# A two-block transformer kernel on one core: its state space mixer in chunks of four tokens, with states at chunk ends and outputs by block matrices

## The chip, the cores and the metric

The kernel runs on one core of a Trainium2 chip. TensorE (PE in the views, PEld for its weight loads) multiplies matrices, VectorE (DVE) and ScalarE (ACT) work on elements, GpSimd (POOL) does a few fills, and SyncE (SP) issues the transfers from HBM. Each engine takes its instructions in order and waits on semaphores where it needs another's result. The metric is the device time of one execution in microseconds, the median of several runs.

## What is computed

256 tokens of width 2048 go through two blocks. The first one has a state space mixer beside a dilated attention, then a feed-forward part; the second one has two kinds of attention and a Fourier mixer. All of it is float32. The mixer takes 1024 of the channels as 64 groups of 16, and each group drives 64 complex states:

```python
bu_re = jnp.einsum('bsgc,gnc->sbgn', uf, bbar_re)
bu_im = jnp.einsum('bsgc,gnc->sbgn', uf, bbar_im)
_, _, h_re, h_im = lax.associative_scan(
    _complex_linear_combine, (a_seq_re, a_seq_im, bu_re, bu_im), axis=0)
y = (jnp.einsum('sbgn,gcn->bsgc', h_re, c_re.astype(f32))
     - jnp.einsum('sbgn,gcn->bsgc', h_im, c_im.astype(f32))
     + d.astype(f32) * uf)
y = jax.nn.gelu(y.reshape(B, S, SSM_WIDTH))
return y * jax.nn.sigmoid(y @ w_glu.astype(f32))
```

So h[t] = a·h[t-1] + B·u[t] for every state, and y[t] = Re(C·h[t]) + d·u[t]. The factor a does not depend on t.

## The kernel before

Nearly all time goes to matrix products whose weights are read once from HBM. A product either runs in float32 (two matmul records in the trace for one 128x512 product) or is split into a high and a low part and run as three products of a faster kind (one record each). The high part is a cast on ACT (`split`, line 177), the low part a subtraction on DVE (line 178).

The side work is written as generators, `Lane`s. A main loop calls `tick()` after every weight tile, and each lane is advanced by its rate in the table `T`: `ada=1.8` and `ssm=5` of a lane's own units at each tick. `ada` streams the modulation weights through DVE (`ada_add`, line 278), one 0.5 MB tile a unit. `ssm` is the mixer. The program order that results is then arranged for each engine by the framework's scheduler, so that rows of different lanes alternate.

Two stages matter here. In stage A (90 to 211 us) the input projection runs, while the modulation columns that it needs are still being computed group by group of channels; the mixer prepares its constants up to the mark "prep". In stage B (211 to 457 us) the rest of the q, k and v products, the dilated attention and one product with w_out run (`rest`, `scores`, `values`, `gemm_full`), and the mixer does its recurrence. At the end of stage B `lanes["ssm"].finish()` stands ahead of the gate product (`ssm_w_glu`), which needs the mixer's y.

The mixer before works on half of the groups (16 pairs of groups, 128 state rows a pair) and 128 tokens at a time, so in four runs:

- `products` (lines 590 to 612) and `expand_b` make, for the taps j = 0 to 3, the matrices a^j·B, transposed so that one matmul sums four tokens.
- `load` (652) copies u for all tokens and all four shifts to `ssm_us`; `inputs` (666) does 32 matmuls of 128x128 weights and 128 columns and copies the result to `ssm_h`. It holds, for each token, the sum of the last four inputs with their powers of a.
- `scan` (676) is then h[t] = a^4·h[t-4] + that sum: 32 steps of four tokens, four DVE instructions of 128 elements each (two products into `ssm_tq`, line 682, two sums into `ssm_h`, line 684).
- `outputs` (689) multiplies every state by C: 32 matmuls with 128x32 weights (`ssm_cl`, made by `expand_c`, 634) and 128 columns, into four column strips; line 698 adds d·u.

## Time and profile before

| | us |
|---|---|
| median of three runs | 2488.83 |
| lowest, highest run | 2485.3, 2496.29 |
| the profiled execution | 2486.17 |
| its span, first to last instruction | 2484.4 |
| PE busy in the span | 2352.2 (95%) |
| DVE busy in the span | 1810.1 (73%) |
| ACT busy in the span | 1124.0 (45%) |
| read from HBM in the span | 587.19 MB, 237 GB/s |

A busy share of the whole span is a mean over stages with different limits. The change lies in the first 460 us, and what it is worth has to be read there: which engine is full in that stretch, and what the idle pieces of that engine waited for.

### The profile page before, as it was taken

What the parts mean: (1) busy time and instruction counts of PE and PEld (TensorE: products, weight loads), DVE (VectorE), ACT (ScalarE), POOL (GpSimd) and SP (SyncE); (2) the same over time, 40 slices, a digit from 0 to 9 for tenths busy, and PEclk for the clock granted to TensorE, in tenths of its full rate; (3) what the DMA queues carried; (4) which work ended last, traced back from release to release, by engine and by line L of the source; (5) the groups of instructions that cost most, each with busy time, mean ns of one, the idle gap of its engine ahead of it and who ended that gap; (6) DMA issues with size and microseconds to landing.
All of it is one profiled execution on the core that took longest, in us unless ns stands there. A gap on an engine that the chain in (4) does not pass through costs nothing.

```text
span 2484.4 us, 30494 instructions
## 1 busy us (share of the span) xinstructions
PE 2352.2 (95%) x10855; PEld 1800.0 (72%) x10855; DVE 1810.1 (73%) x3054; ACT 1124.0 (45%) x1745; POOL 1.4 (0%) x12
## 2 busy tenths in 40 slices
PE   5899999989999999999999999999997999999997
PEld 3455554668887878778777888777776778888886
DVE  5877998787778899876778789646678655555557
ACT  3227752454444333344355455555435445444442
POOL 0000000000000000000000000000000000000000
PEclk9899999999999999999999999999998999999999
DMA  9888778768888878888877988624473765665664
GB/s 290 309 296 307 231 260 285 253 224 291 286 278 273 297 267 291 266 270 280 266 250 222 306 282 291 210 89 162 136 262 115 231 200 176 193 194 157 177 210 138
DMA packets 291538, 591.35 MB, mean 238 GB/s; under 512 B 33733, under 2 KB 56617, under 8 KB 291385
## 3 DMA queue, kind: packets, MB, share of 16 engines
q1 hardware_dynamic: 291384, 589.40, 73.1%
q8 instruction: 85, 1.39, 0.2%
q14 instruction: 69, 0.56, 0.1%
HBM read 587.19 MB, written 2.13 MB: 237 GB/s over the span
## 4 chain that ended last, share of the span: by engine, by line
PE 47%; DMA 22%; DVE 20%; issue 5%; ACT 4%; SPq 1%; DVEq 0%; ACTq 0%
PE mm L133 39%; DMA raw<-in_ada_w_dram 15%; DVE wl L178 6%; DVE acc L278 6%; PE at L133 4%; PE tp L133 2%; DMA raw<-in_w_in_attn_dram 2%; DMA raw<-in_w_ada_dram 2%; ACT ssm_us L663 1%; ACT wh L177 1%; DMA raw<-in_w_ffn_down_dram 1%; PE tp L189 1%; DVE ssm_h L684 1%; DVE ssm_tq L682 1%; DVE wa L278 1%
## 5 line engine op out<-in xcount | busy, mean ns | idle before, releaser
L133 PE MATMUL mm<-wh,s 128*128 128x512 f32 (+3 forms) x4768 | 1462.9, 386 | 2.3 <-ACT wh L177 2.1
L177 ACT CAST wh<-raw 128x1024 fp32r<-128x1024 f32 (+3 forms) x642 | 655.9, 1023 | 896.8 <-PE mm L133 669.9
L133 PEld LDWEIGHTS mm<-wh,s 128*128 128x128 f32 x4768 | 890.2, 189 | 181.1 <-issue 7.8
L178 DVE TENSOR_TENSOR wl<-raw,wh 128x1024 fp32r<-128x1024 f32 (+3 forms) x642 | 755.2, 1185 | 316.6 <-ACT wh L177 311.9
L133 PE MATMUL mm<-wl,s 128*128 128x512 f32 (+3 forms) x2384 | 920.4, 386 | 21.4 <-DVE wl L178 19.6
L278 DVE SCALAR_TENSOR_TENSOR acc<-raw,condT,acc 128x1024 f32<-128x1024 f32 (+2 forms) x413 | 477.7, 1164 | 208.8 <-DMA raw<-in_ada_w_dram 141.9
L133 PEld LDWEIGHTS mm<-wl,s 128*128 128x128 f32 x2384 | 450.5, 189 | 119.7 <-DVE wl L178 33.2
L133 PE MATMUL mm<-wh,sl 128*128 128x512 f32 x608 | 230.9, 475 | 5.1 <-ACT sl L753 2.8
L133 PEld LDWEIGHTS mm<-wh,sl 128*128 128x128 f32 x608 | 112.5, 191 | 68.2 <-issue 41.8
L133 PE MATMUL mm<-wl,sl 128*128 128x512 f32 x368 | 158.2, 494 | 2.6 <-DVE wl L178 2.5
L133 PEld LDWEIGHTS mm<-wl,sl 128*128 128x128 f32 x368 | 67.7, 189 | 52.8 <-issue 38.1
L684 DVE TENSOR_TENSOR ssm_h<-ssm_h,ssm_tq 128x128 f32<-128x128 f32 x256 | 73.2, 286 | 2.5 <-ACT ssm_h L673 1.0
L133 PE MATMUL at<-wl,sl 128*128 128x512 f32 x152 | 68.3, 597 | 1.1 <-DMA wl<-in_w_in_dram 0.5
L133 PE MATMUL tp<-wc,sl 128*128 128x128 f32 (+1 forms) x352 | 49.2, 293 | 18.8 <-ACT wc L837 15.1
L133 PEld LDWEIGHTS tp<-wc,sl 128*128 128x128 f32 x352 | 44.7, 198 | 29.0 <-ACT wc L837 15.4
L682 DVE TENSOR_TENSOR ssm_tq<-ssm_h,ssm_co 128x128 f32<-128x128 f32 x248 | 61.3, 286 | 1.8
L278 DVE SCALAR_TENSOR_TENSOR wa<-raw,condT,wa 128x512 f32<-128x512 f32 (+1 forms) x75 | 48.1, 641 | 11.6 <-DMA raw<-in_w_ada_dram 10.8
L133 PEld LDWEIGHTS at<-wl,sl 128*128 128x128 f32 x152 | 27.7, 190 | 38.7 <-issue 28.6
L133 PE MATMUL at<-s,s 128*128 128x512 f32 (+1 forms) x96 | 42.0, 616 | 3.7 <-ACT wd L1317 3.0
L133 PEld LDWEIGHTS at<-ssm_us,ssm_bl 128*128 128x128 f32 x256 | 30.6, 191 | 11.6 <-ACT ssm_h L673 5.7
L133 PE MATMUL at<-ssm_us,ssm_bl 128*128 128x128 f32 x256 | 34.0, 283 | 3.2 <-ACT ssm_h L673 1.4
L663 ACT COPY ssm_us<-sl 32x512 f32<-32x512 f32 (+3 forms) x56 | 34.4, 615 | 0.9
(330 smaller groups left out, 1588.8 us busy)
## 6 DMA issues: line engine op xcount, KB each, us to landing
raw<-in_w_ada_dram SPq DMA_DIRECT2D x192, 512.0 KB, 5.3
raw<-in_ada_w_dram SPq DMA_DIRECT2D x192, 512.0 KB, 4.8
raw<-in_w_in_fourier_dram SPq DMA_DIRECT2D x128, 512.0 KB, 4.2
raw<-in_w_ffn_gate_dram SPq DMA_DIRECT2D x88, 512.0 KB, 5.0
raw<-in_w_ffn_up_dram SPq DMA_DIRECT2D x88, 512.0 KB, 4.8
raw<-in_w_ffn_down_dram SPq DMA_DIRECT2D x88, 512.0 KB, 5.3
raw<-in_w_in_attn_dram SPq DMA_DIRECT2D x72, 512.0 KB, 5.1
raw<-in_w_out_fourier_dram SPq DMA_DIRECT2D x64, 512.0 KB, 4.2
```

What stands on the lines that cost most here:

```text
L133: PE.matmul(o, l, r, start=start, stop=stop)
L177: S.copy(hi, src)
L178: V.tensor_sub(lo, src, hi.bitcast(F32))
L189: PE.transpose(b[:, o:o + 128], src(c0 + c, t), ident)
L278: V.scalar_tensor_tensor(out=acc, in0=raw, scalar=c, in1=acc, op0=ALU.mult, op1=ALU.add)
L663: copy(d[:, :, z:NT], uT[half][32 * i:32 * i + 32, :, t0 + z - j:t0 + NT - j])
L682: V.tensor_tensor(out=tq, in0=prev[:, c:c + 1].to_broadcast([128, 2, 16, 4]), in1=cof[:, c].unsqueeze(3).to_broadcast([128, 2, 16, 4]), op ...
L684: V.tensor_tensor(out=cur, in0=cur, in1=tq, op=ALU.add)
```

## The change

Both halves of the groups now go through one recurrence, and it keeps only the state at the end of each chunk of four tokens, 64 chunks in all. For that, `chunked` lays u out as 4 tokens x 32 channels on the partitions and 64 chunks in the free dimension, and `inputs` does 64 matmuls of 64 columns in all (128 of 128 columns before). A `scan` step is one product of 128 elements and two sums of 64, with 63 steps in place of 128. Since the states inside a chunk are not there any more, an output needs two things: the chunk's own inputs through a block matrix `tk` of 4x4 blocks C·a^k·B (with d on the diagonal), and the state at the end of the chunk before through the matrices C·a^(j+1), `gx`. `kernel_of` computes the blocks with 32 matmuls for each half (weights 128x128, 32 columns), `chunk_kernel` copies them into place, `outward` and `outward_powers` make C and its powers, and `outputs` does three matmuls of 64 or 63 columns for each of the 32 pairs, with 128x128 weights, and copies the result back to token order in 64 copies of 32 partitions. `products` and `kernel_of` of both halves, and `outward`, now stand ahead of the mark "prep", in stage A. The rates in `T` and everything outside the mixer are as before.

```diff
+        def products(half):
+            pr = slab([128, 4, 256])
+            ex = exs[half] = [w8([128, 16, 4, 2, 16]) for _ in range(2)]
...
+            for j in range(4):
+                d = [pr[:, 2 * (j % 2) + comp] for comp in range(2)]
...
+                for comp in range(2):
+                    for g in range(2):
+                        S.activation(out=ex[comp][:, :, 3 - j, g], in_=f(d[comp]), func=AF.Copy,
+                                     scale=maskb[:, g:g + 1])
+                yield 2.0
+        def outward():
+            for comp in range(2):
+                for half in range(2):
+                    cx = w2([128, 4, 2, 64], "wb")
...
+                    for kk in range(4):
+                        PE.transpose(b[:, kk * 128:(kk + 1) * 128], cx[:, kk].rearrange("p g n -> p (g n)"), ident)
...
+        def kernel_of(half):
...
+            b = ps_at()
+            for q in range(16):
+                for comp in range(2):
+                    mm(b[:, 32 * q:32 * q + 32], exs[half][comp][:, q].rearrange("p j g c -> p (j g c)"),
+                       ct[comp][:, q].rearrange("p g c -> p (g c)"), comp == 0, comp == 1)
...
+        def chunked(half):
+            us[half] = slab([128, 16, 64])
+            for i in range(4):
+                for q in range(4):
...
+                    copy(d, uT[half][32 * q:32 * q + 32, :, i:256:4])
         def inputs(half):
+            for comp in range(2):
+                for h8 in range(2):
+                    b = ps_at()
+                    for q in range(8):
+                        mm(b[:, q * 64:(q + 1) * 64], bls[half][comp][:, 8 * h8 + q], us[half][:, 8 * h8 + q], True, True)
+                    g0 = 16 * half + 8 * h8
+                    S.copy(st[:, :, comp, g0:g0 + 8].rearrange("p n g -> p g n"), b.rearrange("p (g n) -> p g n", g=8))
+        def scan():
+            for c in range(1, 64):
+                cur, prev = st[:, c], st[:, c - 1]
+                tq = sp.tile([128, 2, 2, 32], F32, name=uname("ssm_tq"), tag="ssm_tq")
+                V.tensor_tensor(out=tq, in0=prev.unsqueeze(1).to_broadcast([128, 2, 2, 32]), in1=co, op=ALU.mult)
+                for i in range(2):
+                    V.tensor_tensor(out=cur, in0=cur, in1=tq[:, :, i], op=ALU.add)
+                yield 0.7
+        def outward_powers():
+            for half in range(2):
...
+                for j in range(4):
+                    t1, t2 = temp(), temp()
+                    V.tensor_tensor(out=f(t1), in0=gi, in1=ai, op=ALU.mult)
...
+                            S.activation(out=gx[half][comp][:, :, j, g], in_=g_, func=AF.Copy, scale=maskb[:, g:g + 1])
+        def outputs(half):
+            for h8 in range(2):
+                b = ps_at()
+                for q in range(8):
+                    g = 8 * h8 + q
+                    o = b[:, q * 64:(q + 1) * 64]
+                    mm(o, tk[:, half, g].rearrange("p j c -> p (j c)"), us[half][:, g], True, False)
+                    for comp in range(2):
+                        mm(o[:, 1:64], gx[half][comp][:, g].rearrange("p j g c -> p (j g c)"),
+                           st[:, 0:63, comp, 16 * half + g], False, comp == 1)
                 for i in range(4):
+                    for q in range(4):
+                        copy = (S.copy, V.tensor_copy)[q % 2]
+                        copy(uT[half][32 * q:32 * q + 32, 2 * h8:2 * h8 + 2, i:256:4],
+                             b[32 * i:32 * i + 32].rearrange("p (k q n) -> p q k n", k=2, q=4)[:, q])
+                yield 2.0
+        yield from outward()
+        for half in range(2):
+            yield from products(half)
+            yield from kernel_of(half)
+            if half == 0:
+                yield from expand_b(0)
+        yield "prep"
...
+        for c, cost in enumerate(scan()):
+            yield cost
+            if c % 8 == 2:
+                next(powers, None)
+                yield 2.0
+            if c in (20, 40):
+                chunk_kernel(c // 20 - 1)
...
+        for half in range(2):
+            yield from outputs(half)
```

Where the new work stands is decided by the scheduler, and three places of its order are of use. The first is on PE in stage A, between the 128x512 products of two q, k and v tiles (an `at` buffer is a PSUM bank, `wl` a weight tile). Before:

```order
L133 MATMUL at_801<-wl_847,sl_208 128x512
L133 MATMUL at_802<-wl_847,sl_208 128x512
L133 MATMUL at_859<-wl_861,sl_195 128x512
L133 MATMUL at_860<-wl_861,sl_195 128x512
L133 MATMUL at_859<-wl_871,sl_208 128x512
L133 MATMUL at_860<-wl_871,sl_208 128x512
```

and now, where `wb` is `ct`, `ssm_w` the matrices of `products`, and two rows stand for sixteen pairs of them:

```order
L133 MATMUL at_852<-wl_908,sl_208 128x512
L133 MATMUL at_853<-wl_908,sl_208 128x512
L133 MATMUL at_866<-wb_860,ssm_w_673 128x32
L133 MATMUL at_866<-wb_863,ssm_w_674 128x32
...
L133 MATMUL at_920<-wl_922,sl_195 128x512
L133 MATMUL at_921<-wl_922,sl_195 128x512
```

The 32 matmuls of the first `kernel_of` stand two weight tiles ahead of the end of this group of channels, and they take one of the two `at` banks; those of the second one stand behind the first product of the last group, with no boundary behind them.

The second place is on PE at the mixer's last outputs. Before, they stand inside the first products of the gate (`mm_3698`, whose weights `wh_3702` and `wl_3703` are `ssm_w_glu`), and thirty-two of them follow each other:

```order
L133 MATMUL mm_3698<-wh_3702,sl_3689 128x512
L133 MATMUL mm_3699<-wh_3702,sl_3689 128x512
L133 MATMUL mm_3698<-wl_3703,sl_3689 128x512
L133 MATMUL at_3219<-ssm_h_2412,ssm_cl_2819 32x128
L133 MATMUL at_3219<-ssm_h_2412,ssm_cl_2829 32x128
...
L133 MATMUL mm_3698<-wh_3702,sl_3690 128x512
```

Now, the products with the powers (`ssm_w`) and with the block matrices (the second `ssm_h`) stand among the v products of the second half of the heads:

```order
L133 MATMUL mm_2738<-wh_2824,sl_221 128x512
L133 MATMUL at_2312<-ssm_h_1379,ssm_w_1681 128x63
L133 MATMUL at_2312<-ssm_h_1379,ssm_w_1682 128x63
L133 MATMUL at_2312<-sl_1384,ssm_h_1380 128x64
...
L133 MATMUL mm_2739<-wh_2824,sl_221 128x512
L133 MATMUL mm_2646<-raw_2819,cz 32x512 x2
```

They moved ahead of the second four heads and of the product with w_out, and the whole recurrence has to be done before them. The third place is DVE inside the recurrence, before:

```order
L684 TENSOR_TENSOR ssm_h_2412<-ssm_h_2412,ssm_tq_2910 128x32x4
L684 TENSOR_TENSOR ssm_h_2412<-ssm_h_2412,ssm_tq_2913 128x32x4
L682 TENSOR_TENSOR ssm_tq_2916<-ssm_h_2412,ssm_co 128x128
L682 TENSOR_TENSOR ssm_tq_2919<-ssm_h_2412,ssm_co 128x128
L684 TENSOR_TENSOR ssm_h_2412<-ssm_h_2412,ssm_tq_2916 128x32x4
```

and now:

```order
L713 TENSOR_TENSOR ssm_tq_2280<-ssm_h_1379,ssm_co 128x128
L278 SCALAR_TENSOR_TENSOR acc_2636<-raw_2821,condT,acc_2636 128x1024
L715 TENSOR_TENSOR ssm_h_1379<-ssm_h_1379,ssm_tq_2280 128x64 x2
L713 TENSOR_TENSOR ssm_tq_2284<-ssm_h_1379,ssm_co 128x128
L715 TENSOR_TENSOR ssm_h_1379<-ssm_h_1379,ssm_tq_2284 128x64 x2
```

A step has three instructions that each need the one before, where it had two pairs; `ada_add` (line 278) still stands in between.

## Rows read from the trace of the kernel before

**Rows 1.** Engine busy time by stretch, stages A, B and the rest

```profile
core 0: us, PE busy (x) PEld busy (x) DVE busy (x) ACT busy (x) POOL busy (x), PEclk, DMA share, GB/s
90.00:211.00 121.00, 113.97 (x342) 60.22 (x341) 90.48 (x169) 31.86 (x64) 0.37 (x3) 0.96 0.89 305
211.00:457.40 246.40, 236.90 (x1156) 123.69 (x1154) 222.60 (x797) 136.48 (x312) 0.58 (x4) 0.99 0.79 270
```

**Rows 2.** PE in time inside stage B: start, length, instruction, count

```profile
267.30 3.60 PE L133 MATMUL mm<-wl,sl 128*128 128x512 f32 x8
270.74 7.03 PE L133 MATMUL mm<-wh,sl 128*128 128x512 f32 x16
```

**Rows 3.** What PE waited for in stage B: us, times, longest

```profile
PE tp L189 <- ACT sl L937: 1.6, 2, 1.3
PE at L133 <- ACT ssm_h L673: 1.4, 2, 1.0
PE tp L317 <- ACT wc L314: 0.8, 1, 0.8
```

**Rows 4.** Groups of stage B: count | busy us, mean ns | idle before

```profile
L133 PE MATMUL at<-ssm_us,ssm_bl 128*128 128x128 f32 x256 | 34.0, 283 | 3.2 <-ACT ssm_h L673 1.4 <-issue 0.5 <-DVE sl L698 0.5
L133 PE MATMUL at<-ssm_h,ssm_cl 128*32 128x128 f32 x256 | 9.7, 311 | 0.0
L644 PE MATMUL tp<-ident,wb 128*128 128x128 f32 x16 | 2.3, 276 | 0.0
L682 DVE TENSOR_TENSOR ssm_tq<-ssm_h,ssm_co 128x128 f32<-128x128 f32 x248 | 61.3, 286 | 1.8
L684 DVE TENSOR_TENSOR ssm_h<-ssm_h,ssm_tq 128x128 f32<-128x128 f32 x256 | 73.2, 286 | 2.5 <-ACT ssm_h L673 1.0
L278 DVE SCALAR_TENSOR_TENSOR acc<-raw,condT,acc 128x1024 f32<-128x1024 f32 x52 | 66.4, 1279 | 7.9 <-DMA raw<-in_w_ada_dram 7.8
L604 DVE TENSOR_TENSOR sl<-sl,ssm_t 128x256 f32<-128x256 f32 x4 | 1.7, 423 | 0.0
```

**Rows 5.** DVE in time, one recurrence step and its neighbours

```profile
445.69 0.61 DVE L684 TENSOR_TENSOR ssm_h<-ssm_h,ssm_tq 128x128 f32<-128x128 f32 x2
446.33 0.49 DVE L682 TENSOR_TENSOR ssm_tq<-ssm_h,ssm_co 128x128 f32<-128x128 f32 x2
446.74 0.61 DVE L684 TENSOR_TENSOR ssm_h<-ssm_h,ssm_tq 128x128 f32<-128x128 f32 x2
```

**Rows 6.** DVE, the nearest smaller instruction, from the groups of 90 to 130 us

```profile
L580 DVE TENSOR_TENSOR ssm_p<-ssm_ptmp 128x32 f32<-128x32 f32 x1 | 0.2, 183 | 0.0
```

**Rows 7.** Weight loads in time, for matmuls of one column

```profile
164.62 0.97 PEld L133 LDWEIGHTS tp<-ones,wa 128*128 128x128 f32 x8 [1.20 <-ACT acc L301]
```

**Rows 8.** PE in time in stage A

```profile
97.93 3.70 PE L133 MATMUL at<-wh,sl 128*128 128x512 f32 x8 [0.25 <-DVE sl L800]
112.78 7.13 PE L133 MATMUL at<-wl,sl 128*128 128x512 f32 x16 [0.43 <-DVE sl L800]
164.65 1.02 PE L133 MATMUL tp<-ones,wa 128*128 128x1 f32 x8 [1.15 <-DVE col L748]
169.01 0.79 PE L133 MATMUL mm<-wh,ssm_h 128*128 128x512 f32 x1 [3.34 <-ACT ssm_h L177]
```

**Rows 9.** Busy time and granted clock of one short stretch of stage A

```profile
167.00:175.00 8.00, 5.82 (x15) 4.15 (x16) 7.86 (x14) 6.25 (x13) 0.00 (x0) 0.57 0.80 242
```

**Rows 10.** PE in time at the third and last outputs of the mixer

```profile
405.39 2.02 PE L133 MATMUL at<-ssm_h,ssm_cl 128*32 128x128 f32 x64
...
451.59 0.74 PE L133 MATMUL mm<-wh,sl 128*128 128x512 f32 x2 [1.21 <-ACT wh L177]
453.47 0.51 PE L133 MATMUL mm<-wl,sl 128*128 128x512 f32 x1 [1.14 <-DVE wl L178]
453.90 3.61 PE L133 MATMUL at<-ssm_h,ssm_cl 128*32 128x128 f32 x64
```

## What the change was predicted to do

> **What bounds the kernel now.** I read the busy time by stretch first. The change is inside two stages: A, 90 to 211 us, and B, 211 to 457.4 us. In B, PE is busy 236.9 of 246.4 us and DVE 222.6; transfers run at 270 GB/s there and at 305 GB/s in A [rows 1]. So two engines are nearly full in B, and the share of the whole span would not have told that. A busy PE is not yet a PE at its peak, so next comes PE in time: 8 records of 512 columns start within 3.44 us (267.30 to 270.74) and 16 take 7.03 [rows 2], 0.43 us a record, and this rate returns wherever such products follow each other. PE is thus the engine that sets the end of B, and only its idle 9.5 us (246.4 - 236.9) and a few slow pieces can be taken back by making others faster. Then come its waits: short ones, behind ACT, DVE and transfers, the longest 1.3 us [rows 3]. DVE carries the recurrence, 61.3 + 73.2 = 134.5 us, beside 66.4 us of modulation sums [rows 4]; a step takes 445.69 to 446.74 = 1.05 us [rows 5], 128 steps 134 us.
>
> **DVE, part by part.** A new step has one product of 128 elements and two dependent sums of 64. A 128-element instruction costs 0.25 to 0.29 us (61.3/248, and 73.2/256) [rows 4], one of 32 elements 0.18 [rows 6], so I take 0.22 for 64 elements, and 0.25 + 2 x 0.22 = 0.69 us a step; 63 steps make 43 us, up to 0.8 and 50 us if nothing stands between dependent ones. `outward_powers` adds 48 instructions like line 604, 0.42 us each [rows 4], 20 us, and the copies some 10. DVE's mixer work in B falls from 134.5 to 73-80 us. What that is worth on the clock is only what PE waited for.
>
> **PE in stage B.** Two kinds of product go. The old `inputs` held PE for 34.0 us and the old `outputs` for 9.7 [rows 4]; `expand_c` (16 transposes, 2.3 us of busy time [rows 4], 1.8 us one behind the other) goes to stage A as `outward`. What comes is 64 matmuls of `inputs` and 96 of `outputs`, all with 128x128 weights and at most 64 columns. No row has this shape. Its columns alone would take half of a 128-column record: 34.0/256 = 0.133 us with its waits, so 0.067. The other bound is the weight load: eight one-column records keep it busy for 0.97 us, the last 0.19 of which is latency, so one begins every 0.11 us [rows 7]. With one column there is nothing else to pay, so 64 columns cannot go faster than that, and I take 0.111 us a record, two records a matmul. `inputs`: 128 x 0.111 = 14.2 us. `outputs`: 192 x 0.111 = 21.3 us; the old ones were cheap (9.7/256 = 0.04 us) since their weights have 32 columns. Sum on PE in B: 14.2 + 21.3 - 34.0 - 9.7 - 1.8 = -10.0 us.
>
> The Trainium skill, in "TensorE: Matmul & The Clock Gate", section "Back-to-back issue gap", gives an isolated matmul of up to 64 columns about 25 ns. Rows 7 do not agree: one-column records come every 0.11 us here. By the page's price the new matmuls would fit within the first rival below.
>
> **Waits in stage B.** The last old outputs stand inside the gate product: PE idles 1.21 and 1.14 us there, and they take 3.61 us where the ones before took 2.02 [rows 10]. Now the outputs stand ahead of the second four heads, so the 2.35 us of idle go (the 3.61 is in the 9.7 already). Of the rest (1.6 us behind ACT's scaling of q and k, which waits for DVE's small steps, and 0.8 [rows 3]) I take back 1.5. The 1.4 us for `ssm_h` are a part of the old `inputs`' cover and may return with the new copies; I leave them out. A new wait comes: on PE the first product with the powers needs the end of the recurrence, and the remaining v products, four heads and the product with w_out are queued behind it. Up to there PE has 95 products of 512 columns (2 x 0.43), 64 of `inputs` (0.222), 80 transposes at 0.11, four heads and some 18 small products: about 116 us. DVE has 63 steps (43), 33 modulation sums (42 at 66.4/52 = 1.28 [rows 4]), 40 instructions of 128x256 (17), and some 25 us of copies, norms and head work: 127 us, with the up to 8 us that PE waits elsewhere on the other side. I take 3 us of wait, with 0 and 12 as ends. Stage B: -10.0 - 2.35 - 1.5 + 3 = -10.9 us.
>
> **Stage A.** `kernel_of` adds 64 matmuls there, 128 x 0.111 = 14.2 us (by its 32 columns alone a quarter of the price of 128, at least 3.4). `outward` adds 1.8, hidden: PE waits 0.25, 0.43 and, at the end of a group, about 1 us around there for DVE [rows 8]. The first `kernel_of` (7.1 us) stands two weight tiles ahead of a place where PE idles 1.15 + 3.34 us for the modulation columns [rows 8], which come from HBM, DVE and ACT and do not wait for PE. So 4.5 of its 7.1 us fill that hole. After the hole, the granted clock is 0.57 over 167 to 175 us [rows 9], half speed for most of it; with PE active instead, I take back 2 of the 3.4 us (8 x 0.43) that this costs, with 0 and 3.4 as ends. The second `kernel_of` has no such cover. Each takes one of two `at` banks, so one handover before and one after it, 0.25 to 0.43 us each as between tiles now [rows 8]: 4 x 0.4 = 1.6 us. `products` of the second half (24 instructions of 0.42, 10 us of DVE, moved from B) fits into DVE's 30 idle us of A (121 - 90.5 [rows 1]). ACT is busy 31.9 of 121 there [rows 1], so its new copies cost nothing; without this cover they would be 16 to 20 us. Stage A: 14.2 - 4.5 - 2 + 1.6 = +9.3 us.
>
> **The sum.** -10.9 + 9.3 = -1.6 us, against the profiled execution of 2486.17 us: 2484.6. The median of the runs shown stands 2.66 us higher, so 2487 as a median.
>
> **The rivals.**
> (1) *Weight loads cost less than I take.* If 64 columns set the pace, 320 records cost 0.053 instead of 0.111 and those of `kernel_of` 0.027: 18.6 + 10.7 = 29 us less, 2458. This is the time that the page's price would give. Against it: rows 7.
> (2) *DVE is the real limit of B.* For it: 222.6 of 246.4 us busy. Then all of the idle 9.5 us but the inputs' own 2 goes, and no new wait comes: B is -17.5; with the whole 3.4 us of clock and no bank waits, A is 14.2 - 4.5 - 3.4 = +6.3. Sum -11, 2478. Against it: the PE rate in rows 2.
> (3) *Slower: PE waits for the end of the recurrence.* Place: the first product with the powers. If a step costs 0.9 us, since each of its three instructions needs the one before and modulation sums of 1.28 us stand between them, DVE needs 13 us more than above, PE waits 16, and the sum is +11.5: 2500. It decides against me from about 0.7 us a step, and is over 0.5% from 0.92.
> (4) *Slower: PE reads the states with a stride.* Two of three output matmuls take their 63 columns at steps of 256 bytes, which no row shows. Up to a column time twice the usual, the weight load hides it; at four times, 128 records cost 0.1 us more, +13, 2500.
> The Trainium skill, in "SBUF — State Buffer", section "Door 1: The DMA port swizzle", lets float32 reads stride by up to four elements for free and puts a penalty, without a figure, on each access that goes to a new 16-byte line. The step here is 64 elements, and no run so far shows the price.
> (5) That the change does not do what it says (the recurrence unshortened) is excluded by the order: 63 x 3 instructions in place of 128 x 4.
>
> **How the numbers follow.** My sum 0.55, with 2479 to 2495 from the ends above; rival 1 0.07, rival 2 0.17, rival 3 0.13, rival 4 0.08. The range is 2472 to 2501: below it lie rival 1 and a part of rival 2, above it parts of 3 and 4. A measurement here can tell 0.5%, 12.4 us, from no change: under 2476.4 is faster, over 2501.3 slower. Faster: rival 1, half of rival 2 and a tail of mine, 0.18. Slower: about half of 3 and 4 and a tail, 0.13. The rest, 0.69, is the same.
>
> **What would show it.** Records of `inputs`, `outputs` and `kernel_of` 0.11 us apart (at 0.05 rival 1 holds, at 0.2 rival 4). A step of 0.7 us. DVE in B down by some 55 us. The hole ahead of 169 us gone, and a clock of 1 behind it. PE's work at the gate product without the two waits, and the gate product starting some 2 us earlier. I would be wrong if B shortened by 17 us or more, or if PE stood idle before the first output.

## The result and the profile after

| | before | after |
|---|---|---|
| median, us | 2488.64 | 2518.33 |
| lowest, highest run, us | 2485.3, 2496.29 | 2516.19, 2522.75 |
| the profiled execution, us | 2486.17 | 2516.57 |
| its span, us | 2484.4 | 2514.6 |

The changed kernel is slower: the ratio is 1.0117, with a 95% interval of 1.0089 to 1.0145. I had forecast 2487, with a range that ended at 2501.

The stages moved, so they are read between the same instructions. Stage A ends where the first transposition of the u columns begins: 210.96 us before, 238.58 after. Stage B ends at the gate product; the pair of its products that stood behind the last outputs at 457.4 now starts at 480.04. So A grew by 27.6 us, B shrank by 5.0 (241.5 against 246.5), and 22.6 us of the 30.2 in span are there at the gate. These are the two stages of after by engine (the columns are those of [rows 1]):

```profile
90.00:238.60 148.60, 140.54 (x487) 83.02 (x486) 107.48 (x209) 46.18 (x101) 0.03 (x1) 0.89 0.74 260
238.60:480.00 241.40, 231.51 (x948) 125.31 (x947) 164.05 (x516) 127.26 (x304) 5.38 (x3) 0.97 0.76 261
```

DVE is busy 164.1 us in B, where it was 222.6, and B is only 5.0 us shorter. Stage A has a lower clock than before (0.89 against 0.96) and fewer GB/s (260 against 305), although it does the same loading. PE in time shows where (start, length, instruction, count, idle time before it):

```profile
155.06 8.62 PE L133 MATMUL at<-wb,ssm_w 128*128 128x32 f32 x64
163.49 9.19 PE L133 MATMUL at<-wl,sl 128*128 128x512 f32 x16
...
179.00 1.03 PE L133 MATMUL tp<-ones,wa 128*128 128x1 f32 x8
183.82 0.80 PE L133 MATMUL mm<-wh,ssm_h 128*128 128x512 f32 x1 [3.79 <-ACT ssm_h L177]
...
221.31 9.69 PE L133 MATMUL at<-wb,ssm_w 128*128 128x32 f32 x64
...
238.58 1.04 PE L189 MATMUL tp<-ident,wa 128*128 128x128 f32 x8
...
248.27 13.14 PE L133 MATMUL at<-sl,ssm_w 128*128 128x64 f32 x64 [2.52 <-ACT sl L687]
```

The rows with 128x32 are the two `kernel_of`. They are read with the granted clock of the same stretches, the number behind the five engines:

```profile
150.00:160.00 10.00, 10.00 (x57) 6.86 (x56) 4.33 (x7) 0.00 (x0) 0.00 (x0) 1.00 0.87 305
160.00:170.00 10.00, 10.00 (x33) 6.33 (x33) 6.58 (x10) 2.29 (x5) 0.00 (x0) 0.66 0.25 71
...
220.00:230.00 10.00, 10.00 (x65) 9.22 (x63) 3.68 (x4) 0.00 (x0) 0.00 (x0) 0.79 0.65 249
230.00:240.00 10.00, 10.00 (x38) 8.01 (x38) 5.14 (x5) 3.66 (x7) 1.39 (x2) 0.70 0.33 108
...
250.00:260.00 10.00, 10.00 (x49) 10.00 (x48) 7.42 (x8) 7.68 (x11) 0.00 (x0) 0.50 0.86 311
```

While the 32-column products of `kernel_of` run, the granted clock falls from full speed (2.4 GHz) to half (1.2 GHz), and their 64 records take 8.62 and 9.69 us in place of 7.1. Sixteen 128x512 records behind the first `kernel_of` take 9.19 us where sixteen take 7.03 [rows 2]. The transfers drop to 71 and 108 GB/s. What they wait for is in two rows of DVE in time and two of the queue of transfers (SPq, over 155 to 172 and 217 to 240 us; total us, times, longest):

```profile
163.29 0.69 DVE L675 TENSOR_TENSOR wb<-ident,ssm_ptmp 32x512 f32<-32x512 f32 x1 [5.98 <-PE at L133]
...
230.61 0.69 DVE L675 TENSOR_TENSOR wb<-ident,ssm_ptmp 32x512 f32<-32x512 f32 x1 [6.51 <-PE at L133]
```
```profile
SPq L806 <- DVE wa L278: 8.7, 2, 8.5
SPq L207 <- PE mm L133: 15.3, 2, 13.2
```

DVE's instruction for the diagonal d (line 675 of the changed kernel) writes a `wb` buffer that the products of `kernel_of` still read. DVE takes its instructions in order, so it stands still for 5.98 and 6.51 us, with modulation sums behind it. Around the first `kernel_of` the queue of transfers waits 8.5 us for such a sum to free its tile, around the second one 13.2 us for PE to free a weight tile. PE itself waits for no transfer from the first `kernel_of` to the end of A, so the low rate is not what made A longer. The hole ahead of the first products with `ssm_h`, 3.34 us before [rows 8], is still there with 3.79. At the start of B the first half of `inputs` (64 columns) runs at half clock, 13.14 us for 64 records.

In the rest of B the products and the recurrence went as the working said. Its groups (count | busy us, mean ns | idle before) and the one wait ahead of the outputs (total us, times, longest):

```profile
L133 PE MATMUL at<-sl,ssm_w 128*128 128x64 f32 x128 | 20.7, 337 | 2.5 <-ACT sl L687 2.5
L133 PE MATMUL at<-ssm_h,ssm_w 128*128 128x63 f32 x128 | 20.4, 294 | 1.8 <-DVE ssm_h L715 1.8
L133 PE MATMUL at<-sl,ssm_h 128*128 128x64 f32 x64 | 11.6, 265 | 0.0
L713 DVE TENSOR_TENSOR ssm_tq<-ssm_h,ssm_co 128x128 f32<-128x128 f32 x63 | 18.0, 286 | 2.3 <-ACT ssm_h L697 1.6
L715 DVE TENSOR_TENSOR ssm_h<-ssm_h,ssm_tq 128x64 f32<-128x64 f32 x126 | 27.6, 219 | 1.4
```
```profile
PE at L133 <- DVE ssm_h L715: 1.8, 1, 1.8
```

A step of the recurrence costs 0.286 + 2 x 0.219 = 0.72 us of DVE (0.69 forecast) and PE waits 1.8 us for its end (3 forecast). The two rows of the outputs overlap each other in time; in the timeline six of their records start within 0.67 us, 0.112 each, as forecast.

One forecast for B did not come true. The two waits at the gate product are still there, 2.01 us in place of the 2.35 of [rows 10], although no outputs stand behind them any more:

```profile
478.25 0.73 PE L133 MATMUL mm<-wh,sl 128*128 128x512 f32 x2 [1.30 <-ACT wh L177]
479.70 0.50 PE L133 MATMUL mm<-wl,sl 128*128 128x512 f32 x1 [0.71 <-DVE wl L178]
```

They are waits for the high and the low part of the gate's first weights. PE's idle time in B is 9.9 us (241.40 - 231.51), where it was 9.5.

### The profile page after: what moved, and what is told of

It is laid out like the page before. It is cut to its first block, busy times and chain, and to the rows that moved or that the text cites. A ratio compares the mean times of both kernels' runs of the same rounds, so it can differ in the third digit from the quotient of the medians.

```text
span 2514.6 us, 30153 instructions
## 1 busy us (share of the span) xinstructions
PE 2379.3 (95%) x10791; PEld 1826.3 (73%) x10791; DVE 1768.4 (70%) x2809; ACT 1127.4 (45%) x1770; POOL 5.6 (0%) x7
## 4 chain that ended last, share of the span: by engine, by line
PE 52%; DVE 20%; DMA 18%; issue 5%; ACT 4%; SPq 0%; DVEq 0%; ACTq 0%
PE mm L133 41%; DMA raw<-in_ada_w_dram 14%; PE at L133 7%; DVE wl L178 6%; DVE acc L278 6%; PE tp L133 2%; ACT wh L177 1%; DMA raw<-in_w_ada_dram 1%; DMA raw<-in_w_ffn_down_dram 1%; DMA raw<-in_w_in_attn_dram 1%; PE tp L189 1%; DVE ssm_h L715 1%; DVE wa L278 0%; DVE sl L1570 0%; DVE sl L1573 0%
## 5 line engine op out<-in xcount | busy, mean ns | idle before, releaser
L133 PE MATMUL mm<-wh,sl 128*128 128x512 f32 x536 | 196.2, 459 | 4.5 <-ACT sl L817 2.8
L133 PE MATMUL mm<-wl,sl 128*128 128x512 f32 x440 | 194.9, 521 | 4.3 <-DVE wl L178 2.3
L133 PEld LDWEIGHTS mm<-wh,sl 128*128 128x128 f32 x536 | 100.5, 191 | 56.5 <-issue 32.4
L133 PEld LDWEIGHTS mm<-wl,sl 128*128 128x128 f32 x440 | 82.2, 193 | 68.5 <-issue 51.3
L133 PE MATMUL at<-wl,sl 128*128 128x512 f32 x112 | 52.4, 617 | 0.5 <-DVE sl L864 0.5
L133 PEld LDWEIGHTS at<-wl,sl 128*128 128x128 f32 x112 | 21.3, 198 | 26.6 <-issue 21.5
L133 PE MATMUL at<-wh,sl 128*128 128x512 f32 x80 | 36.0, 597 | 0.0
L457 PE MATMUL tp<-ident,sl 128*128 128x128 f32 x64 | 12.0, 337 | 22.7 <-ACT sl L1594 10.5
L189 PEld LDWEIGHTS tp<-ident,wa 128*128 128x128 f32 x208 | 24.5, 141 | 10.4 <-issue 3.3
L189 PE MATMUL tp<-ident,wa 128*128 128x128 f32 x208 | 30.5, 276 | 0.0
L715 DVE TENSOR_TENSOR ssm_h<-ssm_h,ssm_tq 128x64 f32<-128x64 f32 x126 | 27.6, 219 | 1.4
```

The lines of the kernel that those rows point to most:

```text
L133: PE.matmul(o, l, r, start=start, stop=stop)
L189: PE.transpose(b[:, o:o + 128], src(c0 + c, t), ident)
L457: PE.transpose(b[:, c * 128:(c + 1) * 128], xn(4 * g + c, t), ident)
L715: V.tensor_tensor(out=cur, in0=cur, in1=tq[:, :, i], op=ALU.add)
```

## The experiments

Theory 1: the narrow products cost more than their records, because the clock falls at them and the dear work behind them pays. Theory 2: the added work in A costs its weight loads alone, and the clock falls for another reason. The rival of the prediction that DVE sets the end of B is taken along. The kernel before, timed beside each of them, has medians of 2488.6 to 2490.9. Medians below stand with the lowest and highest run.

**kernel_of with 128 columns.** Each pair writes over a window of four blocks, and later pairs overwrite what is not theirs.

```diff
-                    mm(b[:, 32 * q:32 * q + 32], ..., ct[comp][:, q]..., comp == 0, comp == 1)
+                    e = min(q + 4, 16)
+                    mm(b[:, 32 * q:32 * e], ..., ct[comp][:, q:e]..., comp == 0, comp == 1)
```

> The 64 matmuls of kernel_of take 128 columns of the moving matrix in place of 32 (each later pair writes over the columns that are not its own), so the same weights are loaded as often. Theory 1 (the narrow products lower the granted clock): the half-clock stretches behind the first kernel_of (160.6 to 167.4 us) and around the second (225.5 to 235.7) go, a record stays at 0.112 us, and the time falls by 8 to 10 us, to about 2509. Theory 2 (what was added in stage A costs its weight loads, and the clock falls for another reason, as where PE waits): the clock falls at the same places and the time stays within 3 us of 2518. Theory 3 (columns are paid after all): a record takes over 0.15 us and the time rises.

2499.4 (2491.8 to 2505.4), 19 us less for four times the columns. PE in time and two stretches:

```profile
153.10 7.33 PE L133 MATMUL at<-wb,ssm_w 128*128 128x128 f32 x64
160.26 7.12 PE L133 MATMUL at<-wl,sl 128*128 128x512 f32 x16
...
239.24 13.81 PE L133 MATMUL at<-sl,ssm_w 128*128 128x64 f32 x64 [2.51 <-ACT sl L688]
```
```profile
160.00:170.00 10.00, 9.07 (x34) 4.56 (x32) 9.33 (x16) 5.82 (x11) 0.00 (x0) 1.00 0.88 278
220.00:230.00 10.00, 10.00 (x72) 9.10 (x71) 8.66 (x9) 2.70 (x5) 0.45 (x1) 1.00 0.85 316
```

A record costs 0.112 us with 32 and with 128 columns: the weight load sets it. The clock stays at 1.00, sixteen 512-column records take 7.12 again, the transfers keep 278 GB/s, and stage A ends at 229.56, 9.0 us earlier.

The edit also changed the order on DVE: three more pairs of modulation sums now stand ahead of the diagonal's instruction, which waits 0.5 us there and not 6.0. To tell this from the clock, take each kernel from the start of its first `kernel_of` to the end of A:

```profile
155.06:238.58 83.52, 77.27 (x318) 53.92 (x318) 56.76 (x100) 30.32 (x65) 0.01 (x1) 0.84 0.64 217
153.10:229.56 76.46, 68.96 (x319) 47.20 (x318) 61.00 (x104) 30.57 (x65) 0.01 (x1) 0.93 0.78 262
```

The second row is this run. PE's idle time is no shorter (7.5 us against 6.3), but the same records keep it busy for 8.3 us less. So the gain is the clock's and not that of the DVE order; 2.0 of the 9.0 us had been gained before the first `kernel_of` began, and 1.2 were lost again in waits. Theory 1 holds for A, and not from one profile alone: in the three profiles with 32 columns (the second profile of the changed kernel and the run without the recurrence, both below, are the others) the clock falls at both `kernel_of`, and in this run and the next one, with 128, at none. The other 10 us of the median lie outside A, and this profile alone does not place them.

The Trainium skill, in "TensorE: Matmul & The Clock Gate", section "Back-to-back issue gap", gives an isolated matmul of up to 64 columns about 25 ns. The changed kernel's float32 records with 128x128 weights do not agree: 0.112 us with 32 and with 63 columns.

**Inputs with 128 columns too.**

```diff
-                        mm(b[:, q * 64:(q + 1) * 64], ..., us[half][:, 8 * h8 + q], True, True)
+                        e = min(q + 2, 8)
+                        mm(b[:, q * 64:e * 64], ..., us[half][:, 8 * h8 + q:8 * h8 + e]..., True, True)
```

> As the run with the wide kernel_of, and the 64 matmuls of inputs take 128 columns in place of 64. Theory 1: the first 64 records of inputs take 7.2 us in place of 13.1, the half-clock stretch at 249.4 to 263.0 us goes, and the time is 6 us below the run with the wide kernel_of alone, about 2503. Theory 2 (that stretch comes from the wait of 2.5 us ahead of the inputs, whatever follows it): no difference from the run with the wide kernel_of alone.

2495.4 (2491.8 to 2501.9). The clock still falls behind the 2.5 us wait for the chunk copies, but it comes back soon, as two stretches show:

```profile
239.00:249.00 10.00, 8.08 (x52) 7.54 (x53) 6.36 (x9) 9.78 (x18) 0.00 (x0) 0.83 0.77 270
249.00:259.00 10.00, 8.58 (x76) 8.16 (x75) 7.96 (x22) 9.90 (x28) 0.00 (x0) 1.00 0.55 177
```

So both theories have a part here: the clock falls behind the wait, and narrow products keep it down. The other profiles bear it out. With 64 columns the clock is half for 13 to 17 us in all five; with 128 columns behind this wait it is half for 3 to 4 us in ten of twelve and does not fall in two. The gain of 4 us, of 6 expected, is within the spread of the two sets of runs.

**kernel_of left out.** One product per half fills the bank, so the outputs lack their own chunk's inputs.

> The products of kernel_of are left out (one product per half fills the bank), so the outputs lack the inputs of their own chunk. By the sum over the records of stage A, kernel_of costs 17.9 us itself, 3.8 us in the products behind it and 3.2 us in the second products with the two parts: 25 us, and the time is about 2493. If transfers or the modulation columns were what sets the end of stage A, and the products only stood beside them, the time falls by less than 10 us, to 2508 or more. The hole ahead of the products with the first modulated channels (3.8 us) should stay in any case, since it opens behind PE's own sums with ones.

2499.2 (2491.1 to 2505.4). Stage A ends at 220.8 us, 17.8 earlier than in after, less than the 25 expected, and the hole stays (4.85 us). The median is the same as with the wide form although A is 8.7 us shorter; executions of this kernel lie 14 us apart, and I have a profile of one of the fastest only (2491.6). Where the others lose it stays open.

**The recurrence left out.** The 63 steps are gone, so the states are wrong.

> The 63 steps of the recurrence are left out (189 VectorE instructions, 45 us of its time), so the states are wrong. If TensorE sets the end of stage B, only the wait of 1.8 us ahead of the first product with the powers goes, with up to 2 us more of short waits: 2514 to 2517. If VectorE sets it (rival 2 of the prediction), stage B shortens by more than 5 us: below 2513.

2519.3: nothing gained. Stage B by engine, from the end of A to the gate product:

```profile
236.40:486.70 250.30, 239.01 (x948) 128.16 (x947) 133.15 (x327) 126.00 (x303) 5.43 (x3) 0.96 0.73 256
```

DVE has 133 us of work in place of 164, and PE's idle time is 11.3 us in place of 9.9: PE does not wait for DVE there, so DVE does not set the end of B in the changed kernel. B even took 9 us longer in this profile, most of it with PE busy; why is open. That DVE has time to spare for more work does not follow, as the state layout below suggests.

**The first kernel_of in the hole.** On top of the two wide kinds, the mixer is held before `kernel_of(0)` until the sums with ones of channels 10 to 13 have been issued, and `expand_b(0)` moves ahead of `kernel_of(0)`.

```diff
+            if k0 == 10:
+                lanes["ssm"].until("sums")
+                lanes["ssm"].until("kernel")
+                lanes["ssm"].hold = "prep"
```

> As the run with both kinds of products wide, but the first kernel_of stands behind TensorE's own sums with ones for channels 10 to 13 (172.6 to 174.9 us there) and ahead of the products with these channels, where TensorE idled 3.3 us. If the hole opens only behind those sums, since the columns are made from them, the sums come 7 us earlier, 3.3 us of kernel_of lie in the hole, stage A ends 3 to 4 us earlier (229.3 us there) and the time is about 2492. If the columns come at a time that transfers and VectorE set, as the prediction took it, the products with them cannot start before 178.6 us, and nothing is gained: 2495.

PE in time at the sums:

```profile
165.03 1.03 PE L133 MATMUL tp<-ones,wa 128*128 128x1 f32 x8
165.92 7.31 PE L133 MATMUL at<-wb,ssm_w 128*128 128x128 f32 x64
173.07 0.48 PE L133 MATMUL mm<-wh,ssm_h 128*128 128x512 f32 x1
```

The sums come 8.8 us earlier than with the two wide kinds (165.03 against 173.88), no idle time is left, the products with the new channels start at 173.1 and not at 178.6, and the clock does not fall. Stage A ends at 220.09 against 229.32: 9.2 us, more than the 3 to 4 expected, since the half clock behind the hole went too, and 1.4 us of PE's waits for the copies of `expand_b`. So the columns do wait for PE, through its own sums with ones. The median stayed (2496.5, 2486.9 to 2500.1): the profiled execution is 4.6 us behind the kernel before at 500 us and 13.3 at its end; the clock fell later in it, among other places at 1726 us.

**Operands exchanged.** Weights of 32 columns in four strips and 128 moving columns, then four transposes.

```diff
+                    for i in range(4):
+                        q = 4 * k4 + i
+                        mm(b[32 * i:32 * i + 32, 128 * k4:128 * k4 + 128], ct[comp][:, q]..., exs[half][comp][:, q]..., comp == 0, comp == 1)
...
+                PE.transpose(b[:, 128 * k4:128 * k4 + 128], kt[:, 128 * k4:128 * k4 + 128], ident)
```

> As the run with the first kernel_of in the hole, but kernel_of has its two operands exchanged: weights of 32 columns in four column strips and 128 moving columns, as the outputs of the kernel before had (0.04 us a record), with a copy and four transposes of a 128x128 block behind it (0.11 us each). If weight loads set the price of the 128x128 form (0.112 us a record with 32 and with 128 columns alike), a half takes some 3 us in place of 7.2, the first one lies wholly in the hole, and stage A ends 7 to 8 us earlier than with the wide form: about 2485. If every matmul costs the same whatever its weights, there is no gain: 2492.

PE in time at the exchanged form, and a stretch of stage B with its clock:

```profile
166.53 1.95 PE L133 MATMUL at<-ssm_w,wb 128*32 128x128 f32 x64
```
```profile
362.00:382.00 20.00, 20.00 (x83) 17.60 (x82) 2.97 (x9) 5.93 (x11) 0.00 (x0) 0.50 0.23 80
```

64 records take 1.95 us in place of 7.3, and A ends at 215.3. But the median is 2506.9: at 362 us, in the narrow outputs, the clock was half for 20 us. In this profile the gain in one stage was lost at narrow products of another.

**More main products between the chunk copies and the inputs.**

```diff
         chunked(0)
+        yield 5.0
         inputs(0)
...
         yield from expand_b(1)
+        yield 5.0
         inputs(1)
```

> As the run with the strips, but one more weight tile of the main products is allowed between the copies into chunk layout and the inputs that read them, for both halves. TensorE's wait of 2.5 us for these copies at the beginning of stage B and some of the 3.2 us of waits inside the inputs go, and the clock has no reason to fall there: 3 to 6 us less than the run with the strips, about 2480. If the wait is only moved (ScalarE and VectorE are busy with the same copies whatever stands between), no difference.

2497.4 (2484.8 to 2502.3), not 2480. The wait for the copies stayed at 2.5 us. It is 9.6 us below the run with the strips all the same; in its profile (2484.8 us) the clock holds over the outputs, but that this makes the difference of the medians is not shown.

**Outputs with 126 and 128 columns**, added to the two wide kinds, to the strips, and to the later inputs.

```diff
-                    o = b[:, q * 64:(q + 1) * 64]
+                    n = min(2, 8 - q)
+                    o = b[:, q * 64:(q + n) * 64]
...
-                           st[:, 0:63, comp, 16 * half + g], False, comp == 1)
+                           st[:, 0:63, comp, 16 * half + g:16 * half + g + n]..., False, comp == 1)
```

> As the run with wide kernel_of and inputs, and the 96 matmuls of outputs take 126 and 128 columns in place of 63 and 64; nothing else is moved. In the run with the strips the granted clock was half from 361.8 to 382.3 us, over the narrow outputs. If narrow outputs lower the clock in some executions, the slower ones of the run with two wide kinds (2491.8 to 2501.9) come down, and the median falls from 2495 to about 2491; a record stays at 0.112 us. If the strided read of the states has a price once there are 126 columns, the records take longer and the time rises above 2496. If the outputs never cost clock in that kernel, the median stays within 2 us of 2495.

> As the run with the strips (median 2506.9, clock half for 20.5 us at the outputs in its profile), with the outputs at 126 and 128 columns. If the narrow outputs' clock is what cost that run its gain in stage A (215.3 us for its end, against 220.1 with the wide kernel_of in the hole), the spell goes and the time is 2486 to 2492. If the clock fell there for another reason (a wait ahead of the outputs, the exchanged operands), it falls again and the time stays above 2500.

> As the run with the later inputs (2484.8 to 2502.3, median 2497.4), with the outputs at 126 and 128 columns. If the slower executions of it are those in which the clock fell at the narrow outputs, the median comes near its fastest, 2484 to 2490. If they come from half-clock stretches later in the program, which all kernels here share, it stays at 2494 to 2498.

2507.2, 2503.9 and 2506.9: the first and the third are 12 and 10 us dearer than 2495.4 and 2497.4, the second one is 3 cheaper than 2506.9. The group is from the first of them, and the strided states have their price now: 28.7 us for 112 records (20.4 for 128 above), 0.215 us from one to the next.

```profile
L133 PE MATMUL at<-ssm_h,ssm_w 128*128 128x126 f32 x112 | 28.7, 389 | 0.3 <-DVE ssm_h L718 0.3
```

So a strided column takes about twice a contiguous one (0.215 us for 126, against 0.43 for 512), and at 63 columns it hides under the weight load, which is what the prediction had assumed. The Trainium skill, in "SBUF — State Buffer", section "Door 1: The DMA port swizzle", has a penalty for reads that go to a new line each time; this row agrees, and its figure is the first one here. The strips' two medians differ by less than the spread of either set (2500.5 to 2514.3 and 2495.0 to 2515.1). In the wide one's profile the clock holds over the outputs, so the half clock may have been worth as much as the stride's price there; that is argued, not shown.

**The changed kernel and the later inputs once more**, unaltered.

> The changed kernel once more, unaltered, for a second profile. If the 22.5 us by which it is behind at 500 us come from the narrow products, the clock falls again around both kernel_of and at the first inputs, and it is 21 to 25 us behind there. If the 4.2 us at 1741 to 1751 us belong to the change, the clock falls there again; if that place is chance, it does not, or another one takes its place.

> The kernel with the strips and the later inputs once more, unaltered, for a second profile (its first took 2484.8 us, its other executions up to 2502.3). If its executions differ in the mixer's part, it is more than 5 us behind the kernel before at 500 us, with a half-clock stretch at the narrow outputs; if they differ later, it is within 5 us of it there, and the rest is lost behind 500 us.

2520.1 and 2499.3. In both, the clock was now half over the narrow outputs, where it held in the first profiles; a stretch of each:

```profile
377.00:394.00 17.00, 17.00 (x76) 15.13 (x79) 3.56 (x7) 2.71 (x7) 0.00 (x0) 0.50 0.28 93
```
```profile
352.00:369.00 17.00, 17.00 (x76) 16.04 (x76) 4.37 (x11) 3.32 (x9) 0.00 (x0) 0.50 0.42 147
```

The falls around `kernel_of` and at the first inputs came back in the changed kernel, the one at 1741 us did not. So the clock falls over the outputs in some executions and not in others: in three of the ten profiles with outputs of 63 and 64 columns, in none of the three with 126 and 128 above. The places behind the gate change too. The second profile of the later inputs was 4.5 us behind the kernel before at about 540 us, where the first one was level with it, and 13.1 at its end: within the 5 us of the second outcome, so it lost more behind the mixer than in it. The two profiles of the later inputs are from different chips, so that a chip and an execution are not told apart here; the kernel before took 2489.8 and 2489.9 us on the two.

**States without a stride on PE.** The tile holds the 64 chunks of a pair side by side, and VectorE steps by 256 bytes; on the later and wide form, on all wide kinds alone, and with more products in between.

```diff
-        st = sp.tile([128, 64, 2, 32], ...)
+        st = sp.tile([128, 2, 32, 64], ...)
...
-                cur, prev = st[:, c], st[:, c - 1]
+                cur, prev = st[:, :, :, c], st[:, :, :, c - 1]
```

> As the run with the later inputs and wide outputs (2506.9 us, 0.215 us a record for the strided state reads), but the states lie with the 64 chunks of a pair side by side, so that the outputs read 126 columns without a stride, and the recurrence on VectorE reads and writes one element of every 256 bytes in its place. If the stride is the price, a record of the outputs takes 0.112 us, no half-clock stretch lies over the outputs, and the time is 11 us lower or more: 2487 to 2496. If the stride only changes sides, a step of the recurrence takes over 1.1 us in place of 0.7, TensorE waits more than 10 us for its end, and the time stays above 2500.

> The changed kernel with all three kinds of products wide and with that layout, nothing moved and no operands exchanged: what the narrow products cost as a whole. From the first two runs (2499.4 and 2495.4) and a half-clock stretch of 17 us over the outputs in the second profile of the changed kernel (8.5 us), I expect 2488 to 2495, 24 to 30 us below the changed kernel's 2518. If the outputs' clock was chance that costs little on average, it stays at 2495.

> As the run with the layout (kernel_of exchanged and in the hole, everything wide), with more of the main products between the copies into chunk layout, the inputs and the transposes, so that TensorE need not wait 2.5 us each for the copies and for expand_b. If these waits are then covered, 4 to 6 us below the run with the layout, and below the kernel before's 2489. If ScalarE is the limit there, the waits stand elsewhere and there is no difference.

2504.7, 2511.4 and 2503.2. PE's records are back at 0.112 us, but DVE pays; groups of the first kernel:

```profile
L728 DVE TENSOR_TENSOR ssm_h<-ssm_h,ssm_tq 128x64 f32<-128x64 f32 x126 | 34.4, 273 | 1.9
L726 DVE TENSOR_TENSOR ssm_tq<-ssm_h,ssm_co 128x128 f32<-128x128 f32 x63 | 23.5, 373 | 1.0
L133 PE MATMUL at<-ssm_h,ssm_w 128*128 128x126 f32 x112 | 19.3, 301 | 3.2 <-DVE ssm_h L728 3.2
```

A step takes 0.92 us, 12 us more in sum, and PE idles for DVE and for ACT work behind it. The stride only changed sides, though not by as much as the second outcome had. In the first kernel the outputs start at 360.8 us, at 349.9 with the strided states, from the same end of A (215.5 and 215.6); PE's 9.4 us less on them make up for most of it, and the medians 2504.7 and 2506.9 agree within the spread. So here 12 us more on DVE cost about what the stride had, where taking all 45 us away had gained nothing. The second kernel (2511.4) says less: its profile was 7.2 us behind the strided one already at the end of A, which the layout does not touch. More products in between moved the waits, with no gain beyond the spread.

**Only the block matrices wide.** Their moving columns lie side by side, so a third of the outputs' records can take 128 or 256 columns without a stride (on the later inputs).

```diff
+                    n = min(2, 8 - q)
-                    mm(o, tk[:, half, g]..., us[half][:, g], True, False)
+                    mm(b[:, q * 64:(q + n) * 64], tk[:, half, g]..., us[half][:, g:g + n]..., True, False)
```

> As the run with the later inputs (2497.4 us; in its second profile the clock was half for 17 us over the outputs), but the products with the block matrices, a third of the outputs' 192 records, take 128 columns side by side in place of 64; the two with the strided states keep 63, so that no record gets dearer. If the narrow outputs cost clock in some executions and a third of wide records is enough, the median falls by 3 to 8 us, to 2489 to 2494. If it is not enough, or the outputs cost nothing on average, it stays at 2495 to 2500.

> The same with 256 columns for the products with the block matrices: 64 records at 0.22 in place of 0.111 us, 7 us less a few narrower ones, some 5 us more of columns. If the clock over the outputs is worth more than that, it comes out below 2497; if the clock already holds with 128 columns, 5 us above the run with 128; if the outputs cost no clock, 2502.

2489.0 with 128, a ratio to the kernel before of 1.000 (0.998 to 1.002), and 2493.9 with 256, dearer by about what the columns cost, as the second outcome had it, though the two sets overlap (2477.3 to 2497.5 and 2488.3 to 2501.6). In the profile of the first the clock holds over the outputs:

```profile
349.00:378.00 29.00, 27.88 (x224) 24.68 (x221) 19.46 (x49) 13.96 (x33) 0.00 (x0) 1.00 0.73 245
```

It holds in the profile with 256 too, and it had held in the first profile of the later inputs without any wide record. So the kernel is 8 us faster than the later inputs and level with the kernel before; that the clock over the outputs makes the 8 us is not shown.

**The same with still more products between.** The first of four such changes:

```diff
         chunked(0)
-        yield 5.0
+        yield 15.0
         inputs(0)
...
```

> As the run with the block products at 128 columns (2489.0 us), with more of the main products allowed between the copies into chunk layout, the inputs and the transposes of the second half. TensorE waits 2.5 us for these copies and 2.5 us for the transposes' there. If only the place of these instructions makes the waits, 3 to 5 us less: 2484 to 2486. If ScalarE's and VectorE's copies are the limit at the beginning of stage B, the wait stands elsewhere, at the q and k products' transposes, and the time stays at 2488 to 2491.

2500.9 (2500.0 to 2504.5), above both outcomes. The wait stands elsewhere, and it is longer; and at the outputs, behind two more waits (1.8 and 1.3 us), the clock was half again. PE in time, and a stretch:

```profile
237.36 0.48 PE L189 MATMUL tp<-ident,sl 128*128 128x128 f32 x1 [4.98 <-ACT sl L1028]
```
```profile
359.00:383.00 24.00, 24.00 (x103) 21.74 (x104) 9.20 (x27) 6.33 (x17) 0.00 (x0) 0.50 0.42 142
```

So a third of wide records is no guarantee. Whether it is the waits ahead that decide is not shown: the profile with 256 columns had 2.0 us of wait there and kept its clock.

## Why the prediction was wrong

The sum was -1.6 us, measured +30.2 in span: 31.8 us off, and four terms carry it.

- **Clock at kernel_of: 9.0 us, not in the sum at all.** I priced 64 narrow matmuls by their records (14.2 us) and used the clock only once, as something that more work would give back (-2). Shown by the wide `kernel_of`: the same records, clock 1.00, A ends 9.0 us earlier, with PE busy 8.3 us less from the first `kernel_of` to the end of A.
- **The hole of 4.5 us, and the half clock behind it: 9.2 us.** The step that failed reads: the columns "do not wait for PE". The 3.34 us begin behind PE's own sums with ones, through DVE and ACT, so work ahead of those sums only moves them. Shown by the run with `kernel_of` in the hole. The sum had taken 6.5 of these 9.2 us (4.5 and 2) as won; the rest is waits that grew, among them 1.4 us for the copies of `expand_b`. 9.0 and 9.2 make the 18.3 by which A missed (27.6 against 9.3).
- **Clock at the first inputs: 6.0 us.** 13.14 against the 7.1 that 64 records cost. The wide inputs show the mechanism; the size is from the row. Without it B would be at -11.0, beside a forecast of -10.9, but that is luck. The "2.35 us of idle" at the gate product did not go: they are waits for the gate's own weights, and 2.01 are left. The wait of 2.5 us for the chunk copies was left out. PE's idle time in B grew by 0.4 us where the sum had -0.85, and its busy time fell by 1.4 us more than forecast, once the 6.0 are taken off (5.4 + 6.0 against 10.0).
- **Behind the gate: 7.6 us**, where I had none. At 1741 us, where PE waited 2.2 us, the clock fell in the first profile of after and not in the second, which was 32.9 us behind at 500 us and 33.9 at its end. From 1741 to 1751 us it was 0.51, by estimate 5 of the 7.6; the rest has no place yet. Chance of an execution, as far as these runs show; I did not settle it.

What held: outputs at 0.112 us a record (21.3 us forecast), the recurrence at 0.72 us a step, 1.8 us of wait for its end. By the last sign of the prediction, PE idle before the first output, that wait would have spoken against it, but the sum itself had 3 us of it. Of the rivals, cheap weight loads (1) fell by the record price, DVE as the limit (2) by the run without the recurrence, PE waiting for the recurrence (3) by the 1.8 us. Rival 1's 2458 is not what the 25 ns cited from the Trainium skill ("TensorE: Matmul & The Clock Gate", section "Back-to-back issue gap") would give, as the prediction has it: at 25 ns a record the estimate is about 2449. The 0.112 us answers both. The stride (4) had the right price, twice a column, and by its own rule stayed hidden. That it ended on the slower side had none of these reasons: no rival let the added products touch the clock, though [rows 9] had shown what half speed costs.

## What to carry to other kernels

A product with few columns and full weights costs its weight load, so widening it up to that load costs nothing, and here it kept the clock: price narrow products by what runs behind them too. A hole that opens behind an engine's own instruction can be filled only from behind that instruction. An instruction that writes a buffer which the added products still read holds up everything behind it on its engine, here the modulation sums and through them the transfers. A wait is taken back only by what it waits for: the two at the gate product stayed when the outputs left. Time taken from an engine that isn't the limit bought nothing here, but that does not mean that one may add to it.

## What was not expected of the hardware

- Records of float32 with 128x128 weights: 0.112 us with 32, 64 and 128 columns side by side and with 63 at steps of 256 bytes; 0.215 with 126 at such steps. With weights of 32 columns in four strips, 64 records in 1.95 us.
- On DVE, single elements at steps of 256 bytes took 0.273 us for 64 (0.219 side by side) and 0.373 for 128 (0.286).
- The same program had the clock at 1.00 over its narrow outputs in one execution and at half for 17 us in another. Behind a wait of 2.5 us it stayed at half for 13 to 17 us over records of 64 columns, for 3 to 4 us over records of 128.
